# FFN-down projection: weight panels by column chunk, one sum of the seven-product square taken by an accumulating transfer, and four more squares

## The chip, the cores and the metric

The kernel runs on one core of a Trainium2 chip. The metric is the device time in microseconds (us) of one execution; lower is better. The engines named here are PE (matmul), DVE (vector), ACT (scalar), POOL (GpSimd) and SP (issues transfers).

## What is computed

One decoder layer over 256 tokens of width 2048, in float32. The change concerns the channel mixer:

```python
h2 = rms_norm(x, mlp_norm[i])
x = x + jnp.square(jax.nn.relu(h2 @ w_ffn_up[i])) @ w_ffn_down[i]   # 2048 -> 8192 -> 2048
gate = jax.nn.sigmoid(rms_norm(x, ple_norm[i]) @ w_ple_gate[i])
x = x + gate * (p[i] @ w_ple_proj[i])
```

## The kernel before

**Split numbers.** Each float32 operand is split into a high part `wh` (ACT copies it to the matmul's type, 512 columns at a time) and a low part `wl` (DVE subtracts the copy from the original). A product of two split operands takes three matmuls, high x high, high x low, low x high, on 128x512 tiles. Raw weights come as panels of 128x1024 (512 KB) by transfers that SP issues in order (`load_raw`, L158); six buffers go round, three in each of two pools.

**The down projection.** The hidden width 8192 is worked in two halves (`hf` 0 and 1), each after its part of the up projection. A half has two sweeps (`pair` 0 and 1, 1024 output columns each), so there are four: d00, d01, d10, d11. A sweep runs over 16 steps `kp`. A step multiplies a 2x2 block of activation tiles (a11, a12, a21, a22; two token tiles by two tiles of 128 hidden channels) with a 2x2 block of weights (w11, w12, w21, w22; two tiles of hidden channels by two chunks of 512 columns). It does so in one of two ways:

- A *classic* step takes eight products, 24 matmuls. Its two panels are each split once, into `wh`/`wl` a and b.
- A *square* takes seven products (Winograd's form of Strassen's scheme), 21 matmuls. It needs sums of the weight blocks (`td`, t1 to t4, by DVE, L1269 to L1272), and these are split as well: `wh`/`wl` b for the second panel, c and d for the sums, `wad` for w11. It also needs sums of the activations, S, made once in each half in the up projection (`activation_sums`).

Squares are the steps in `SEVEN` = (1, 3, 5, 7, 9, 11, 13) in d00, d01 and d10, and (1, 3, 7, 11) in d11: 25 of 64. The other steps are classic. Eight banks of PSUM collect the products over the sweep; after its last square the sums of banks go into the residual `x`, scaled by `s2` (L1249).

**Buffers.** `wh`/`wl` of kinds a, b and c go round three tiles each, d two in all (`graw`, which the kept gate panels share in d11), `wad` and `td` have one each. A conversion waits until PE has done with what stood in its tile, and a panel's load waits until the last instruction that reads its buffer's old panel is through.

**Order.** Apart from the part up to the output projection, a scheduler sets the order on each engine from the program's order and priorities; conversions have a high priority. Each engine runs its instructions strictly in that order, and SP too.

Of the kernel before, what the change touches and what calls it, by code (L numbers as in the profile page):

```python
# [9 lines left out]
F32 = mybir.dt.float32  # L10
F32R = mybir.dt.float32r
# [29 lines left out]
def trunk(  # L41
# [1114 lines left out]
    def inv_ms():  # L1156
        ss2 = rms_stat(xr, "n2")
        nc.vector.tensor_scalar(s2, ss2, 1.0 / D, NORM_EPS, op0=ALU.mult, op1=ALU.add)
        nc.vector.reciprocal(s2, s2)

# [27 lines left out]
    SEVEN = (1, 3, 5, 7, 9, 11, 13)  # L1188
    s_slots = (0, 2, 5)

    def activation_sums(box, kp, r):

        i = SEVEN.index(kp)
        if i % 2 == 0:
            st = a8(s_slots[i // 2], f"S{kp}", F32R) if i < 6 else fp.tile([128, 1024], F32R, tag="S", name=f"S{kp}")
            box[kp] = box[SEVEN[min(i + 1, len(SEVEN) - 1)]] = st
# [5 lines left out]
        nc.vector.tensor_tensor(s3, a11, a21, op=ALU.subtract)  # L1202
# [4 lines left out]
    def down_sweep(hf, pair, ys, sboxes, hooks=(), between=None, seven=SEVEN):  # L1207

        nm = f"d{hf}{pair}"
        hooks = dict(hooks)  # L1210
# [37 lines left out]
        def add(tt, c, src):  # L1248
            nc.vector.scalar_tensor_tensor(xs(tt, c), src, s2[:, tt : tt + 1], xs(tt, c), op0=ALU.mult, op1=ALU.add)  # L1249

        for q, kp in enumerate(((0, 2, 1, 4, 3, *range(5, 16)) if hf else (0, 2, 1, 4, 3, 6, 5, 8, 7, 10, 9, 12, 11, 14, 13, 15)) if pair else range(16)):
# [4 lines left out]
            rx, ry = (load_raw(w_down[pair, hf * 32 + 2 * kp + i], 1024, f"{nm}_{kp}_{i}") for i in range(2))  # L1256
            if kp in seven:
                i = SEVEN.index(kp)
                st = sboxes[kp][:, i % 2 * 1024 : i % 2 * 1024 + 1024]
                s1, s2_, s3, s4 = ((st[:, c * 128 : c * 128 + 128], st[:, 512 + c * 128 : 640 + c * 128]) for c in range(4))  # L1260
                t_ = a8(1, f"t{nm}_{kp}")
                t1, t3, t2, t4 = (t_[:, c * 512 : c * 512 + 512] for c in range(4))
                wa = fp.tile([128, 1024], F32R, tag="wa", name=f"wa{nm}_{kp}")
                w11 = wa[:, 0:512], wa[:, 512:1024]
                with tc.high_priority(20000):
                    split_sb(*w11, rx[:, 0:512])
                w21, w22 = halves_of(ry, f"{nm}_{kp}b")
                with tc.high_priority(20000):
                    nc.vector.tensor_tensor(t1, rx[:, 512:1024], rx[:, 0:512], op=ALU.subtract)  # L1269
                    nc.vector.tensor_tensor(t3, ry[:, 512:1024], rx[:, 512:1024], op=ALU.subtract)  # L1270
                    nc.vector.tensor_tensor(t2, t3, rx[:, 0:512], op=ALU.add)
# [213 lines left out]
```

## Time and profile before

| what | value |
|---|---|
| median of 3 runs | 1182.05 us (1179.92 to 1183.51) |
| span of the profiled execution | 1177.7 us (that execution's total time is not given) |
| busy PE, DVE, ACT, POOL | 1162.0, 872.0, 710.5, 13.9 us |
| sweeps d00 and d01, from the first matmul | 556.90 and 639.19 us |
| sweeps d10 and d11, from the first matmul | 899.9 and 982.2 us |
| HBM read | 213.59 MB |

The span runs from the first to the last instruction. Numbers of buffers are left out of names in the trace, so `wl_d_5c` is the low part of kind c at step 5 in any sweep. In a row of the timeline the columns are start, duration, engine, line, operation, out<-in, shapes, and in brackets the idle time before it and what ended that.

### The profile page before, as it was taken

The page shows a single profiled execution, that of the slowest core. Times are in us where ns is not written, and L with a number is a line of the kernel's source. Part 1 is how long each engine was busy: PE and PEld are TensorE (multiplying, and loading weights), DVE is VectorE, ACT ScalarE, POOL GpSimd, SP SyncE. Part 2 cuts the span into 40 slices and gives each one's busy share as a digit, 9 for nine tenths or more (in the row PEclk, how much of TensorE's full clock was granted, in tenths as well). Part 3 has the DMA queues.
Part 4 walks back from the last instruction along what each step waited for, and adds up shares of the span by engine and source line. Part 5 has one row for each costly group of instructions (what it writes and reads, how often), then busy time and mean ns, then how long its engine had stood idle before and what let it go on. Part 6 is the DMA issues. An engine that isn't in the chain of part 4 may idle for free.

```text
span 1177.7 us, 17287 instructions
## 1 busy us (share of the span) xinstructions
PE 1162.0 (99%) x6419; PEld 973.2 (83%) x6419; DVE 872.0 (74%) x1184; ACT 710.5 (60%) x1313; POOL 13.9 (1%) x73
## 2 busy tenths in 40 slices
PE   9999999999999999999999999999999999999997
PEld 8787777788887888888888888888888888888886
DVE  7686996954756666767988987666678979788543
ACT  8776858676545465555665664555556655668544
POOL 2100000000000000000000000000000000000000
PEclk9999999999999999999999999999999999999999
DMA  8464443354555555556556556555555556767511
GB/s 292 158 199 144 140 146 109 119 179 162 175 186 176 179 182 194 193 185 209 185 198 210 206 199 203 194 184 195 182 194 190 206 206 196 291 227 249 196 54 72
DMA packets 60756, 216.81 MB, mean 184 GB/s; under 512 B 6784, under 2 KB 7552, under 8 KB 60288
## 3 DMA queue, kind: packets, MB, share of 16 engines
q1 hardware_dynamic: 60240, 215.12, 54.3%
q8 instruction: 50, 0.82, 0.3%
q10 hardware_dynamic: 432, 0.60, 0.1%
q14 instruction: 34, 0.28, 0.1%
HBM read 213.59 MB, written 2.10 MB: 183 GB/s over the span
## 4 chain that ended last, share of the span: by engine, by line
PE 94%; ACT 2%; DVE 2%; DMA 1%; SPq 0%; issue 0%; DVEq 0%; ACTq 0%
PE u_w L1112 20%; PE u_w L1117 10%; PE d_b L1230 7%; PE d_b L1231 7%; PE d_b L1229 7%; PE d_w L1230 2%; PE d_w L1231 2%; PE d_w L1229 2%; PE gt_b L242 2%; PE gt_b L241 2%; PE gt_b L238 2%; PE o_b L241 1%; PE o_b L242 1%; PE zv_b L238 1%; PE o_b L238 1%; PE zp_b L238 1%
## 5 line engine op out<-in xcount | busy, mean ns | idle before, releaser
L1112 PE MATMUL u_w<-h,wh_u 128*128 128x512 f32 x1024 | 321.9, 396 | 0.0
L167 ACT ACTIVATE wh_u<-raw_u 128x512 fp32r<-128x512 f32 x256 | 147.5, 623 | 160.9 <-issue 98.2
L168 DVE TENSOR_TENSOR wl_u<-raw_u,wh_u 128x1024 fp32r<-128x1024 f32 x128 | 156.6, 1224 | 105.0 <-ACT wh_u L167 103.3
L1117 PEld LDWEIGHTS u_w<-h,wl_u 128*128 128x128 f32 x1024 | 192.4, 188 | 45.4
L1117 PE MATMUL u_w<-h,wl_u 128*128 128x256 f32 x1024 | 201.4, 278 | 0.0
L1112 PEld LDWEIGHTS u_w<-h,wh_u 128*128 128x128 f32 x1024 | 156.0, 189 | 0.1
L168 DVE TENSOR_TENSOR wl_gt<-raw_gt,wh_gt 128x1024 fp32r<-128x1024 f32 x24 | 29.4, 1224 | 23.2 <-ACT wh_gt L167 23.2
L167 ACT ACTIVATE wh_gt<-raw_gt 128x512 fp32r<-128x512 f32 x48 | 28.0, 638 | 23.1 <-PE gt_b L242 14.4
L241 PE MATMUL gt_b<-wh_gt,h 128*128 128x512 f32 x96 | 37.3, 389 | 0.0
L242 PE MATMUL gt_b<-wh_gt,h 128*128 128x512 f32 x96 | 37.3, 389 | 0.0
L168 DVE TENSOR_TENSOR wl_o<-raw_o,wh_o 128x1024 fp32r<-128x1024 f32 x16 | 19.6, 1223 | 12.9 <-ACT wh_o L167 9.9
L167 ACT ACTIVATE wh_o<-raw_o 128x512 fp32r<-128x512 f32 x32 | 18.4, 623 | 16.3 <-issue 8.4
L167 ACT ACTIVATE wh_zp<-raw_zp 128x512 fp32r<-128x512 f32 x32 | 18.6, 624 | 15.8 <-PE zp_b L242 7.2
L168 DVE TENSOR_TENSOR wl_zk<-raw_zk,wh_zk 128x1024 fp32r<-128x1024 f32 x16 | 19.4, 1222 | 9.2 <-ACT wh_zk L167 9.2
L241 PE MATMUL zv_b<-wh_zv,hTh 128*128 128x512 f32 x64 | 26.0, 406 | 0.0
L241 PE MATMUL zp_b<-wh_zp,hTh 128*128 128x512 f32 x64 | 25.7, 401 | 0.0
L238 PE MATMUL gt_b<-wl_gt,h 128*128 128x512 f32 x96 | 25.7, 389 | 0.0
L168 DVE TENSOR_TENSOR wl_zv<-raw_zv,wh_zv 128x1024 fp32r<-128x1024 f32 x16 | 19.5, 1221 | 8.2 <-ACT wh_zv L167 7.3
L241 PE MATMUL zk_b<-wh_zk,hTh 128*128 128x512 f32 x64 | 25.2, 394 | 0.3 <-ACT wh_zk L167 0.3
L241 PE MATMUL zr_b<-wh_zr,hTh 128*128 128x512 f32 x64 | 25.4, 397 | 0.0
L167 ACT ACTIVATE wh_zk<-raw_zk 128x512 fp32r<-128x512 f32 x32 | 18.4, 623 | 11.0 <-PE zv_b L242 4.0
L242 PE MATMUL zp_b<-wh_zp,hTl 128*128 128x512 f32 x64 | 25.0, 391 | 0.0
(837 smaller groups left out, 2964.2 us busy)
## 6 DMA issues: line engine op xcount, KB each, us to landing
raw_u<-in_w_ffn_up_dram SPq DMA_DIRECT2D x128, 512.0 KB, 3.5
raw_d<-in_w_ffn_down_dram SPq DMA_DIRECT2D x128, 512.0 KB, 4.3
raw_gt<-in_w_ple_gate_dram SPq DMA_DIRECT2D x24, 512.0 KB, 3.5
raw_zk<-in_w_in_dram SPq DMA_DIRECT2D x16, 512.0 KB, 3.6
raw_zr<-in_w_in_dram SPq DMA_DIRECT2D x16, 512.0 KB, 3.3
raw_zv<-in_w_in_dram SPq DMA_DIRECT2D x16, 512.0 KB, 3.4
raw_zp<-in_w_in_dram SPq DMA_DIRECT2D x16, 512.0 KB, 3.3
raw_o<-in_w_out_dram SPq DMA_DIRECT2D x16, 512.0 KB, 4.0
```

The lines of the kernel that those rows point to most:

```text
L167: nc.scalar.activation(wh[:, a * 512 : (a + 1) * 512], raw[:, a * 512 : (a + 1) * 512], AF.Copy)
L168: nc.vector.tensor_tensor(wl, raw, wh.bitcast(F32), op=ALU.subtract)
L238: nc.tensor.matmul(banks[tt], ah[:, ts_], halves[a][1], start=False, stop=last)
L241: nc.tensor.matmul(banks[tt], ah[:, ts_], halves[a][0], start=i + a == 0, stop=False)
L242: nc.tensor.matmul(banks[tt], al[:, ts_], halves[a][0], start=False, stop=False)
L1112: nc.tensor.matmul(bank[:, ct, :].rearrange("p (s t) -> p s t", s=2), wh[:, cs[ct]], hl, start=k == 0, stop=False, skip_group_check=True,)
L1117: nc.tensor.matmul(bank[:, ct, 0:T], wl[:, cs[ct]], hl[:, 0, :], start=False, stop=k == 15, skip_group_check=True)
L1229: nc.tensor.matmul(banks[n], ah, wh, start=first, stop=False)
L1230: nc.tensor.matmul(banks[n], ah, wl, start=False, stop=False)
L1231: nc.tensor.matmul(banks[n], al, wh, start=False, stop=last)
```

## The change

- The weights of the down projection are laid out by column chunk: the first panel of a step holds [w21, w11], the second [w22, w12], instead of one panel for each tile of hidden channels.
- In a square, after the second panel has landed, POOL issues an accumulating transfer that adds w11 from memory to the panel's half with w12 (256 KB). The panel then holds w22 and w11 + w12.
- One DVE subtraction of 512 columns makes t2 = (w11 + w12) - w22, and one of 1024 columns makes [w21 - t2, w11 - t2]. Before there were four of 512. Signs are changed: s3 is negated, and the sums that it enters are added with `ns2` = -`s2`.
- Both panels are split whole (a and b), the pair of differences is d, and t2 goes through `wad`. Kind c is gone.
- `SEVEN` becomes (1, 3, 4, 6, 8, 9, 11, 13), eight squares in d00, d01 and d10; d11 takes (1, 3, 6, 9, 11). That makes 29 of 64. The second sweeps run over the steps in another order (`visits`).
- The order of the products in a square changes (6, 4, 7 at the end), and classic steps take the panels by column chunk.
- `phl` of the next stage takes the tile of the last S.

```diff
-    SEVEN = (1, 3, 5, 7, 9, 11, 13)
+    SEVEN = (1, 3, 4, 6, 8, 9, 11, 13)
...
-        nc.vector.tensor_tensor(s3, a11, a21, op=ALU.subtract)
+        nc.vector.tensor_tensor(s3, a21, a11, op=ALU.subtract)
...
+        visits = (range(16), (0, 2, 1, 5, 3, 4, 7, 6, 10, 8, 9, 12, 11, 14, 13, 15))[pair] if seven is SEVEN else (0, 2, 1, 4, 3, *range(5, 16))
...
+        def panel(kp, c, name):
+            return load_raw(w_down[pair, hf * 16 + kp, c].rearrange("p r n -> p (r n)"), 1024, name)
...
-            rx, ry = (load_raw(w_down[pair, hf * 32 + 2 * kp + i], 1024, f"{nm}_{kp}_{i}") for i in range(2))
+            rx, ry = (panel(kp, c, f"{nm}_{kp}_{c}") for c in range(2))
...
+                nc.gpsimd.dma_start(ry[:, 512:1024], w_down[pair, hf * 16 + kp, 0, :, 1, :], accum_op=ALU.add)
                 t_ = a8(1, f"t{nm}_{kp}")
-                t1, t3, t2, t4 = (t_[:, c * 512 : c * 512 + 512] for c in range(4))
+                t2, t43 = t_[:, 0:512], t_[:, 512:1536]
                 wa = fp.tile([128, 1024], F32R, tag="wa", name=f"wa{nm}_{kp}")
-                w11 = wa[:, 0:512], wa[:, 512:1024]
+                w2 = wa[:, 0:512], wa[:, 512:1024]
+                w21, w11 = halves_of(rx, f"{nm}_{kp}a")
+                w22, w1 = halves_of(ry, f"{nm}_{kp}b")
                 with tc.high_priority(20000):
-                    split_sb(*w11, rx[:, 0:512])
-                w21, w22 = halves_of(ry, f"{nm}_{kp}b")
-                with tc.high_priority(20000):
-                    nc.vector.tensor_tensor(t1, rx[:, 512:1024], rx[:, 0:512], op=ALU.subtract)
-                    nc.vector.tensor_tensor(t3, ry[:, 512:1024], rx[:, 512:1024], op=ALU.subtract)
-                    nc.vector.tensor_tensor(t2, t3, rx[:, 0:512], op=ALU.add)
-                    nc.vector.tensor_tensor(t4, ry[:, 0:512], t2, op=ALU.subtract)
-                w1, w3 = halves_of(t_[:, 0:1024], f"{nm}_{kp}c")
-                w2, w4 = halves_of(t_[:, 1024:2048], f"{nm}_{kp}d", True)
-                for n, a_, w_ in (("1", a11, w11), ("2", a12, w21), ("3", s4, w22), ("5", s1, w1), ("7", s3, w3), ("6", s2_, w2), ("4", a22, w4)):
+                    nc.vector.tensor_tensor(t2, ry[:, 512:1024], ry[:, 0:512], op=ALU.subtract)
+                    nc.vector.tensor_tensor(
+                        t43.rearrange("p (r n) -> p r n", r=2), rx.rearrange("p (r n) -> p r n", r=2),
+                        t2.unsqueeze(1).to_broadcast([128, 2, 512]), op=ALU.subtract,
+                    )
+                    split_sb(*w2, t2)
+                w4, w3 = halves_of(t43, f"{nm}_{kp}d", True)
+                for n, a_, w_ in (("1", a11, w11), ("2", a12, w21), ("3", s4, w22), ("5", s1, w1), ("6", s2_, w2), ("4", a22, w4), ("7", s3, w3)):
                     prod(n, a_, w_)
...
-                    add(0, 1, u)
+                    add(0, 1, u, ns2)
...
-            down_sweep(hf, 1, ys, sboxes, {5: keep, 8: keep, 11: keep, 14: keep}, lambda: [h3_part("ple_norm", n) for n in range(2)], (1, 3, 7, 11))
+            down_sweep(hf, 1, ys, sboxes, {5: keep, 8: keep, 11: keep, 14: keep}, lambda: [h3_part("ple_norm", n) for n in range(2)], (1, 3, 6, 9, 11))
...
-    ph, pl = (fp.tile([128, 512], F32R, tag=nm, name=nm) for nm in ("ph", "pl"))
+    phl = fp.tile([128, 2048], F32R, tag="S", name="phl")
+    ph, pl = phl[:, 0:512], phl[:, 512:1024]
...
-        "w_ffn_down": a["w_ffn_down"][0].reshape(64, 128, 2, 1024).transpose(2, 0, 1, 3),
+        "w_ffn_down": a["w_ffn_down"][0].reshape(32, 2, 128, 2, 2, 512)[:, ::-1].transpose(3, 0, 4, 2, 1, 5),
```

What this does to the order of instructions is seen best on DVE. In the names, `raw_d00_8_1` is the second panel of step 8 in sweep d00 (0 is the first), `td` holds the sums of a square's weights, `wl_d00_8a` is the low part of kind a, and the last number is the buffer's. DVE in sweep d00 before, from square 5 to the beginning of square 7:

```order
L1269 TENSOR_TENSOR td00_5_5627<-raw_d00_5_0_5623 128x512
L1270 TENSOR_TENSOR td00_5_5627<-raw_d00_5_1_5625,raw_d00_5_0_5623 128x512
L1271 TENSOR_TENSOR td00_5_5627<-td00_5_5627,raw_d00_5_0_5623 128x512
L1241 TENSOR_TENSOR wl_d00_4a_5590<-raw_d00_4_0_5585,wh_d00_4a_5589 128x1024
L173 TENSOR_TENSOR wad00_5_5628<-raw_d00_5_0_5623,wad00_5_5628 128x512
L1241 TENSOR_TENSOR wl_d00_4b_5607<-raw_d00_4_1_5587,wh_d00_4b_5606 128x1024
L1272 TENSOR_TENSOR td00_5_5627<-raw_d00_5_1_5625,td00_5_5627 128x512
L1241 TENSOR_TENSOR wl_d00_5b_5632<-raw_d00_5_1_5625,wh_d00_5b_5631 128x1024
L1241 TENSOR_TENSOR wl_d00_5d_5646<-td00_5_5627,wh_d00_5d_5645 128x1024
L1241 TENSOR_TENSOR wl_d00_5c_5641<-td00_5_5627,wh_d00_5c_5640 128x1024
L1269 TENSOR_TENSOR td00_7_5713<-raw_d00_7_0_5709 128x512
L1270 TENSOR_TENSOR td00_7_5713<-raw_d00_7_1_5711,raw_d00_7_0_5709 128x512
```

The sums of a square stand between the conversions; each reads panels that have landed, and t1 needs the first panel alone.

DVE in sweep d00 now, from square 8 to the second panel of it (the subtraction of 9 is in between, since 8 and 9 are adjacent squares):

```order
L1276 TENSOR_TENSOR td00_8_5767<-raw_d00_8_1_5764 128x512
L1277 TENSOR_TENSOR td00_8_5767<-raw_d00_8_0_5762,td00_8_5767 128x1024
L1244 TENSOR_TENSOR wl_d00_7a_5729<-raw_d00_7_0_5724,wh_d00_7a_5728 128x1024
L1244 TENSOR_TENSOR wl_d00_7b_5746<-raw_d00_7_1_5726,wh_d00_7b_5745 128x1024
L1244 TENSOR_TENSOR wl_d00_8a_5770<-raw_d00_8_0_5762,wh_d00_8a_5769 128x1024
L173 TENSOR_TENSOR wad00_8_5768<-td00_8_5767,wad00_8_5768 128x512
L1244 TENSOR_TENSOR wl_d00_8d_5784<-td00_8_5767,wh_d00_8d_5783 128x1024
L1276 TENSOR_TENSOR td00_9_5814<-raw_d00_9_1_5811 128x512
L1277 TENSOR_TENSOR td00_9_5814<-raw_d00_9_0_5809,td00_9_5814 128x1024
L1244 TENSOR_TENSOR wl_d00_8b_5775<-raw_d00_8_1_5764,wh_d00_8b_5774 128x1024
```

Both subtractions of square 8 (L1276 reads the half that the added transfer completes) stand ahead of the two conversions of classic step 7, and those of 9 ahead of the second panel of 8.

The same queue further on, from square 11 to the first panel of step 12:

```order
L1276 TENSOR_TENSOR td00_11_5899<-raw_d00_11_1_5896 128x512
L1244 TENSOR_TENSOR wl_d00_10b_5878<-raw_d00_10_1_5858,wh_d00_10b_5877 128x1024
L1277 TENSOR_TENSOR td00_11_5899<-raw_d00_11_0_5894,td00_11_5899 128x1024
L1244 TENSOR_TENSOR wl_d00_11a_5902<-raw_d00_11_0_5894,wh_d00_11a_5901 128x1024
L173 TENSOR_TENSOR wad00_11_5900<-td00_11_5899,wad00_11_5900 128x512
L1244 TENSOR_TENSOR wl_d00_11d_5916<-td00_11_5899,wh_d00_11d_5915 128x1024
L1244 TENSOR_TENSOR wl_d00_11b_5907<-raw_d00_11_1_5896,wh_d00_11b_5906 128x1024
L1276 TENSOR_TENSOR td00_13_5984<-raw_d00_13_1_5981 128x512
L1277 TENSOR_TENSOR td00_13_5984<-raw_d00_13_0_5979,td00_13_5984 128x1024
L1244 TENSOR_TENSOR wl_d00_12a_5946<-raw_d00_12_0_5941,wh_d00_12a_5945 128x1024
```

Here one conversion of step 10 follows the subtraction of 11, and the conversions of step 12 follow both subtractions of 13.

DVE at the start of d00, now, right behind the first subtraction of square 1 (`r7` and `y7` belong to the end of the up projection):

```order
L1277 TENSOR_TENSOR td00_1_5465<-raw_d00_1_0_5460,td00_1_5465 128x1024
L1244 TENSOR_TENSOR wl_d00_0a_5427<-raw_d00_0_0_5422,wh_d00_0a_5426 128x1024
L173 TENSOR_TENSOR wad00_1_5466<-td00_1_5465,wad00_1_5466 128x512
L1244 TENSOR_TENSOR wl_d00_1d_5482<-td00_1_5465,wh_d00_1d_5481 128x1024
L1244 TENSOR_TENSOR wl_d00_0b_5444<-raw_d00_0_1_5424,wh_d00_0b_5443 128x1024
L1244 TENSOR_TENSOR wl_d00_1a_5468<-raw_d00_1_0_5460,wh_d00_1a_5467 128x1024
L1321 TENSOR_TENSOR r7_1_5410<-u7_w1_5317,r7_1_5410 128x512
L1322 SCALAR_TENSOR_TENSOR r7_1_5410<-r7_1_5410 128x512
L1244 TENSOR_TENSOR wl_d00_1b_5473<-raw_d00_1_1_5462,wh_d00_1b_5472 128x1024
L173 TENSOR_TENSOR y7_5217<-r7_1_5410,y7_5217 128x512
L1276 TENSOR_TENSOR td00_3_5550<-raw_d00_3_1_5547 128x512
L1244 TENSOR_TENSOR wl_d00_2a_5512<-raw_d00_2_0_5507,wh_d00_2a_5511 128x1024
```

The first subtraction of square 3 has moved ahead of the conversion of step 2's first panel; both stand behind square 1.

POOL after its last copy of the earlier stages, now (before, nothing followed there; `in_w_ffn_down_dram` is the weights in memory); the list goes on in the same way through the four sweeps:

```order
L804 COPY tE_t_2736<-AR1_1500 128x6x64 x2
L1268 DMA raw_d00_1_1_5462<-in_w_ffn_down_dram 128x512
L1268 DMA raw_d00_3_1_5547<-in_w_ffn_down_dram 128x512
L1268 DMA raw_d00_4_1_5594<-in_w_ffn_down_dram 128x512
L1268 DMA raw_d00_6_1_5679<-in_w_ffn_down_dram 128x512
L1268 DMA raw_d00_8_1_5764<-in_w_ffn_down_dram 128x512
```

Each of them waits for its panel's landing, and the DVE subtraction of L1276 waits for it.

24 lines of the change are left out of this document (13 added, 11 removed).

## The prediction

> **What bounds the kernel now.** I read the page's head and chain first: whether one engine carries the span.
>
> ```profile
> span 1177.7 us, 17287 instructions
> PE 1162.0 (99%) x6419; PEld 973.2 (83%) x6419; DVE 872.0 (74%) x1184; ACT 710.5 (60%) x1313; POOL 13.9 (1%) x73
> PE 94%; ACT 2%; DVE 2%; DMA 1%; SPq 0%; issue 0%; DVEq 0%; ACTq 0%
> ```
>
> PE carries the span. Then the busy times by stretch, for the four sweeps of the down projection (start:end, length, busy time of each engine).
>
> ```profile
> core 0: us, PE busy (x) PEld busy (x) DVE busy (x) ACT busy (x) POOL busy (x), PEclk, DMA share, GB/s
> 556.90:639.20 82.30, 82.30 (x366) 68.14 (x365) 71.37 (x83) 49.68 (x86) 0.00 (x0) 1.00 0.58 199
> 639.20:726.00 86.80, 86.80 (x390) 71.96 (x389) 76.42 (x87) 51.40 (x89) 0.00 (x0) 1.00 0.58 200
> 890.00:987.00 97.00, 97.00 (x444) 80.78 (x443) 86.06 (x100) 58.08 (x102) 0.00 (x0) 1.00 0.58 201
> 987.00:1060.00 73.00, 73.00 (x331) 60.26 (x330) 60.80 (x68) 47.17 (x87) 0.00 (x0) 1.00 0.70 249
> ```
>
> PE has no hole in any sweep, at full granted clock, and DVE runs beside it at 87 to 89% in the first three. Nothing else can become faster than PE's own instruction count allows; anything that comes late costs its full lateness. What one matmul costs is the spacing of starts, not the row's duration (matmuls overlap): first matmul of sweep d00 and first of d01.
>
> ```profile
> 556.90 0.40 PE L1229 MATMUL d_b<-wh_d_0a,y 128*128 128x512 f32 x1
> ...
> 639.19 0.39 PE L1229 MATMUL d_b<-wh_d_0a,y 128*128 128x512 f32 x1
> ```
>
> Between them lie 7 squares of 21 matmuls and 9 classic steps of 24, 363 in all: 82.29 / 363 = 0.2267 us each. A square is 4.76 us, a classic step 5.44 us, one product 0.68 us.
>
> **What the change takes from PE.** Squares go from 7+7+7+4 to 8+8+8+5, four more. Each replaces 24 matmuls by 21: 12 x 0.2267 = 2.7 us, the whole possible gain, 0.23%. Comparisons of this kernel tell about 0.3% (3.5 us) from no change.
>
> **What it takes from the converters.** One period of d00 on DVE, kp 5 (square) to kp 7 (the numbers in brackets are idle time):
>
> ```profile
> 581.48 1.23 DVE L1241 TENSOR_TENSOR wl_d_5c<-td,wh_d_5c 128x1024 fp32r<-128x1024 f32 x1 [1.17 <-ACT wh_d_5c L1240]
> 582.74 0.69 DVE L1269 TENSOR_TENSOR td<-raw_d 128x512 f32<-128x512 f32 x1
> 583.35 0.68 DVE L1270 TENSOR_TENSOR td<-raw_d,raw_d 128x512 f32<-128x512 f32 x1
> 584.07 0.69 DVE L1271 TENSOR_TENSOR td<-td,raw_d 128x512 f32<-128x512 f32 x1
> 584.68 1.22 DVE L1241 TENSOR_TENSOR wl_d_6a<-raw_d,wh_d_6a 128x1024 fp32r<-128x1024 f32 x1
> 585.81 0.69 DVE L173 TENSOR_TENSOR wad<-raw_d,wad 128x512 fp32r<-128x512 f32 x1
> 586.41 1.22 DVE L1241 TENSOR_TENSOR wl_d_6b<-raw_d,wh_d_6b 128x1024 fp32r<-128x1024 f32 x1
> 587.55 0.69 DVE L1272 TENSOR_TENSOR td<-raw_d,td 128x512 f32<-128x512 f32 x1
> 588.15 1.22 DVE L1241 TENSOR_TENSOR wl_d_7b<-raw_d,wh_d_7b 128x1024 fp32r<-128x1024 f32 x1
> ```
>
> Back to back a 512-column instruction takes 0.62 us of the queue and a 1024-column one 1.14. A square costs DVE five of the first and three of the second before, 6.5 us, and two and four after, 5.8 us; a classic step stays at 2.3. A sweep: 7 x 6.5 + 9 x 2.3 = 66 before, 8 x 5.8 + 8 x 2.3 = 65 after. ACT converts seven halves a square as before. The converters are no tighter over a sweep, and since PE never waits for them this saves nothing.
>
> Small things, at nothing:
>
> ```profile
> L1201 DVE TENSOR_TENSOR s<-r x14: 291/293/294, 404.6 to 881.4; 128x128 f32<-128x128 f32 x14
> L1158 DVE TENSOR_SCALAR s2sq<-ss_n x1: 164/164/164, 440.7 to 440.7; 128x2 f32<-128x2 f32 x1
> L168 DVE TENSOR_TENSOR wl_u<-raw_u,wh_u 128x1024 fp32r<-128x1024 f32 x128 | 156.6, 1224 | 105.0 <-ACT wh_u L167 103.3
> ```
>
> One more square in each half means one more set of activation sums, four of 0.29 us and a split, and once `ns2` at 0.16 us, all in the up projection, where DVE idles 105 us before `wl_u`. If that cover were gone they would cost 4 us. `phl` in the place of S waits for square 11's last product, some 20 us before it is needed.
>
> **What it adds: a transfer in series.** Per square, POOL waits for the second panel, issues an accumulating transfer of 256 KB into half of it, and DVE's first subtraction waits for that landing. POOL has nothing else to do there (0.00 in the stretches), so nothing is queued behind it but the next such transfer. Behind the subtraction on DVE, though, stand conversions that PE needs sooner, and the panel's buffer is freed later. Loads have no spare start: SP waits for the buffers.
>
> ```profile
> SPq L158 <- DVE wl_d_8a L1241: 23.9, 4, 6.3
> SPq L158 <- DVE wl_d_9b L1241: 8.7, 4, 4.7
> ```
>
> The issue waits up to 6.3 us for `wl_d_8a` to be done (us in total, times, longest). Six buffers go round, so the second panel of square n is issued when `wl` b of three steps earlier is done. The price X of the added transfer, from the issuable moment to landing, is in no row. Nearest rows (KB, median us to landing):
>
> ```profile
> raw_u<-in_w_ffn_up_dram SPq DMA_DIRECT2D x128, 512.0 KB, 3.5
> raw_d<-in_w_ffn_down_dram SPq DMA_DIRECT2D x128, 512.0 KB, 4.3
> gu<-in_g_up_dram SPq DMA_DIRECT2D x2, 256.0 KB, 4.2
> wa<-in_wa_up_dram SPq DMA_DIRECT2D x2, 256.0 KB, 2.8
> raw_pT<-in_pT_dram SPq DMA_DIRECT2D x1, 256.0 KB, 3.8
> ```
>
> Plain 256 KB transfers take 2.8 to 4.2 us. The new one adds a read of its destination, issued from another engine, so I keep 2.8 as the low end; for the high end, 5.0, the 4.2 of `gu` plus the 0.8 by which `raw_d` in a crowd exceeds `raw_u`. I take X = 3.8, the row of `raw_pT`: that size, in this part of the program, between panel loads. A panel load spaced from others is 3.5.
>
> **The place that repeats.** The pattern in d00 is 7 classic, 8, 9 squares, 10 classic, 11 square, 12 classic, 13 square; t2 is the first subtraction. Suppose t2 of 8 starts at s, late enough that PE waits for `wl_d00_7a` behind it. That ends at s + 0.62 + 1.14 + 1.2, and with 0.1 of signalling PE starts 7 at s + 3.05. It starts 9 at T = s + 3.05 + 5.44 + 4.76 = s + 13.25. DVE goes on without a break through `wl_d00_8b`, ten instructions, 3 x 0.62 + 7 x 1.14: done at s + 9.8 = T - 3.45. That frees the buffer for 11's second panel: landed T + 0.05, summed T + 0.05 + X. Does t2 of 11 wait? The instruction ahead, `wl_d00_9d`, follows an ACT conversion that waits for PE to finish 8, as here:
>
> ```profile
> 580.29 1.15 ACT L1240 ACTIVATE wh_d_5c<-td 128x512 fp32r<-128x512 f32 x2 [1.58 <-PE d_b L1231]
> ```
>
> So DVE is free at T + 0.3 + 1.15 + 1.2 = T + 2.7; the sum comes at T + 3.85. With 0.12 of signalling, t2 and `wl_d00_10b` end at T + 5.8, and 13's second panel is loaded: landed T + 9.35, summed T + 13.15; t2 of 13 starts at T + 13.25 and `wl_d00_12a` is ready 3.05 later, T + 16.3. PE is through 9, 10, 11 at T + 4.76 + 5.44 + 4.76 = T + 14.96. It waits 1.35 us. In general the wait is 2 (3.5 + X) - 13.25: zero at X = 3.1, twice as steep as X. It falls on 7 and 12 in d00 and in d10 and on the two like places in d01: 6 x 1.35 = 8.1 us.
>
> **The starts of sweeps.** In d00 the second panel of square 1 is what DVE waited for even before; its first reader:
>
> ```profile
> L1270 DVE TENSOR_TENSOR td<-raw_d,raw_d x25: 682/684/694, 549.3 to 1027.6; 128x512 f32<-128x512 f32 x25
> ```
>
> t2 now starts at 549.3 + 3.8 = 553.1; six instructions later `wl_d00_0b` is done at 558.9, which frees the buffer for square 3: landed 562.4, summed 566.2. `wl_d00_2a`, behind t2 of 3, is ready at 568.1, and PE wants it at 556.90 + 5.44 + 4.76 = 567.1: 1.0 us. From there seven DVE instructions to `wl_d00_3b` (both subtractions of 4 stand before it) end at 576.3, wanted at 575.0: 1.3 us. Twice, for d00 and d10: 4.6 us. In d01 and d11 the first squares come later, with 1 us more room in the same two round trips (2 x 7.3 - 14.2 = 0.4 us each); in d11 a one-round place gives 0.2 and square 11, whose last product shares buffers with the kept gate panels, 0.5. Together 1.5 us.
>
> **Sum.** -2.7 + 8.1 + 4.6 + 1.5 = +11.5 us. The page gives the span, 1177.7, and no total of that execution; the median of the runs is 4.3 above it, and I put the sum on the median, 1182.05: 1193.5.
>
> **Rivals.** *The transfer is hidden.* If X is at most 3.1, the repeating wait is gone, and at 2.8 only 0.5 in d11 remains: 1182.05 - 2.7 + 0.5 = 1179.9. For it: `wa` at 2.8, an idle POOL, DMA share of only 0.58. Against: the other two rows of that size. Decided at X = 3.1. The Trainium skill (DMA: Bandwidth & Descriptors, Anatomy of one DMA, SWDGE path) puts a transfer issued from POOL at about 2.0 us plus its bytes over 436 GB/s, which would be an estimated 2.6 us here and lead to this case; no run so far shows a transfer issued from POOL, and the rule says nothing of accumulation.
>
> *The transfer is much slower.* At X = 5 the repeating wait is 3.75, six times 22.5; the starts 7.5 for d00 and d10; d01 about 3, d11 about 5: 38 - 2.7 = +35, 1217. For it: 29 more transfers, 7.6 MB, on a queue share already at 0.58 to 0.70, and each reads and writes SBUF.
>
> *DVE becomes the bound by adjacent squares* (3, 4 and 8, 9), with X small: two squares cost DVE 11.6 us against PE's 9.5. But conversions run a step ahead, and over the five-step period DVE needs 22 of 25.2 us; it costs at most the 1.3 us at `wl_d00_3b` twice.
>
> **How the numbers follow.** Forecast case (X from 3.1 to 4.6, 0 to +27 us): 0.5. Hidden: 0.35, kept that high since the walk turns on a margin of 0.7 us in X. Much slower: 0.15. Hidden gives -2 us, a quarter of it read as faster: 0.09 faster, 0.26 same. Of the forecast case 0.07 lies under +3.5 (X below 3.3). So 0.09, 0.33, 0.58. The range takes in the hidden case with a run's scatter, 1177.5, and goes up to X = 4.5 (repeating wait 2.75, 16.5; starts 7.5; d01 and d11 5): 1209, with 5 for panel loads slowed by the traffic: 1214.
>
> **What would show it.** Right: PE idle in front of the products with `wh_d_7a`, `wh_d_12a` (d00), `wh_d_2a`, `wh_d_3b`, ended by DVE `wl_d`; DVE idle before L1276 ended by DMA `raw_d`; POOL's transfers near 3.8 us. Wrong: PE without holes in the sweeps and those transfers under 3.1; or, if PE waits while they are under 3.1, my walk of the queues. PE's matmuls must be 12 fewer in any case.

## The result, and the profile after

| | before | after |
|---|---|---|
| median of 4 runs each | 1182.35 us (1179.92 to 1183.51) | 1274.77 us (1271.28 to 1275.74) |
| ratio, 95% interval | | 1.0781 [1.0767, 1.0795] |
| span of the profiled execution | 1177.7 us | 1269.6 us |
| mean granted clock over the span | 0.998 | 0.976 |

The change costs 92 us. The forecast had 11, with 1214 as its upper end. The page of the changed kernel: head, granted clock by slices, the new queue, the shares of the chain (the work that ended last, followed back from the end), and the group of t2, the subtraction that reads the summed panel (busy, mean ns | idle before it, what ended it).

```profile
span 1269.6 us, 17391 instructions
PE 1190.7 (94%) x6407; PEld 985.4 (78%) x6407; DVE 871.9 (69%) x1161; ACT 716.6 (56%) x1327; POOL 39.1 (3%) x102
PEclk9999999999999999999888999999998998999999
q0 software_dynamic: 4176, 7.60, 3.7%
PE 71%; DMA 11%; DVE 8%; issue 7%; ACT 2%; SPq 0%; DVEq 0%; POOLq 0%; ACTq 0%
L1276 DVE TENSOR_TENSOR td<-raw_d 128x512 f32<-128x512 f32 x29 | 20.1, 692 | 106.9 <-DMA raw_d<-in_w_ffn_down_dram 83.4
```

PE has 12 matmuls fewer, and DVE is as busy as before (871.9 against 872.0), but it stands idle 106.9 us in front of t2, and the chain, once 94% PE, now goes through DMA, DVE and issue for 26%. Before, the four subtractions of all squares had 4.6 us of idle time in front of them, most of it at the first of them:

```profile
L1269 DVE TENSOR_TENSOR td<-raw_d 128x512 f32<-128x512 f32 x25 | 17.3, 692 | 2.4 <-DMA raw_d<-in_w_ffn_down_dram 1.8
```

In the two pairs of sweeps (stretch, length, busy times, granted clock, DMA share) PE no longer runs without holes:

```profile
557.50:763.50 206.00, 171.68 (x691) 136.01 (x690) 139.88 (x141) 100.16 (x177) 13.05 (x15) 0.93 0.60 178
946.60:1165.00 218.40, 189.39 (x785) 151.04 (x784) 154.19 (x163) 115.10 (x208) 10.45 (x12) 0.94 0.63 200
```

One wait, in sweep d00, step by step. PE first:

```profile
603.01 0.39 PE L1232 MATMUL d_b<-wh_d_7a,y 128*128 128x512 f32 x1
609.20 0.80 PE L1233 MATMUL d_b<-wl_d_7a,y 128*128 128x512 f32 x1 [5.80 <-DVE wl_d_7a L1244]
```

PE wants the low part of the first panel of step 7, a classic step. ACT had made the high part of it by 598.98:

```profile
597.84 1.14 ACT L1243 ACTIVATE wh_d_7a<-raw_d 128x512 fp32r<-128x512 f32 x2
```

So the panel had long landed. As far as the trace tells, DVE could have made `wl_d_7a` at 599.7, when it was through with `wl_d_6b`. Instead:

```profile
598.44 1.22 DVE L1244 TENSOR_TENSOR wl_d_6b<-raw_d,wh_d_6b 128x1024 fp32r<-128x1024 f32 x1
606.05 0.69 DVE L1276 TENSOR_TENSOR td<-raw_d 128x512 f32<-128x512 f32 x1 [6.40 <-issue]
606.78 1.22 DVE L1277 TENSOR_TENSOR td<-raw_d,td 128x1024 f32<-128x1024 f32 x1
607.92 1.22 DVE L1244 TENSOR_TENSOR wl_d_7a<-raw_d,wh_d_7a 128x1024 fp32r<-128x1024 f32 x1
```

t2 of square 8 is ahead of it in the queue and waits 6.4 us for the accumulating transfer, which POOL began at 598.72 and which landed at 605.97 ("issue" here means that the profile names no releaser; the landing is 0.08 us ahead of the start):

```profile
598.72 0.87 POOL L1268 DMA_DIRECT2D raw_d<-in_w_ffn_down_dram  x1 [12.33 <-DVE wl_d_6d L1244]
```

In 24 of the 29 squares t2 starts within 0.1 us of its transfer's landing. DVE's wait for these landings, and the three largest waits of PE, which end at low parts that stood behind a t2 (engine, what it waited for, us in total, times, longest):

```profile
DVE td L1276 <- DMA raw_d<-in_w_ffn_down_dram: 83.4, 18, 8.8
PE d_b L1233 <- DVE wl_d_7a L1244: 8.2, 2, 5.8
PE d_b L1233 <- DVE wl_d_2a L1244: 8.0, 2, 4.0
PE d_b L1233 <- DVE wl_d_12a L1244: 7.3, 2, 4.9
```

And the clock. The stretch inside and behind that wait (its columns as above, the granted clock third from the end):

```profile
600.00:606.40 6.40, 3.40 (x15) 2.45 (x14) 0.35 (x1) 1.17 (x3) 0.00 (x0) 1.00 0.49 125
607.00:610.30 3.30, 1.10 (x3) 0.91 (x4) 3.30 (x4) 1.62 (x3) 0.62 (x1) 0.50 0.58 84
610.50:617.00 6.50, 6.50 (x23) 5.17 (x23) 5.79 (x6) 1.28 (x3) 0.00 (x0) 0.75 0.70 239
```

Half the clock is granted from 607.0 to 613.8, 6.8 us; matmuls start 0.43 us apart there in place of 0.2267. The two pairs of sweeps have 12 such stretches, of 3.4 or 6.8 us.

The account, from the starts of successive matmuls: 27 gaps over 0.7 us cost 67.5 us beyond the usual spacing (36.8 in d00 and d01, 30.7 in d10 and d11), the matmuls at slower spacing some 25 us, 12 fewer matmuls give 2.7 back: some 90 of the 91.9 us between the spans.

### The profile page after: what moved, and what is told of

It reads as the page before. It is cut to its first block, busy times and chain, and to the rows that moved or that the text cites. A ratio compares the mean times of both kernels' runs of the same rounds, so it can differ in the third digit from the quotient of the medians.

```text
span 1269.6 us, 17391 instructions
## 1 busy us (share of the span) xinstructions
PE 1190.7 (94%) x6407; PEld 985.4 (78%) x6407; DVE 871.9 (69%) x1161; ACT 716.6 (56%) x1327; POOL 39.1 (3%) x102
## 3 DMA queue, kind: packets, MB, share of 16 engines
q0 software_dynamic: 4176, 7.60, 3.7%
## 4 chain that ended last, share of the span: by engine, by line
PE 71%; DMA 11%; DVE 8%; issue 7%; ACT 2%; SPq 0%; DVEq 0%; POOLq 0%; ACTq 0%
PE u_w L1112 17%; DMA raw_d<-in_w_ffn_down_dram 9%; PE u_w L1117 9%; PE d_b L1233 3%; PE d_b L1234 3%; PE d_b L1232 3%; PE gt_b L242 2%; PE gt_b L238 2%; PE gt_b L241 2%; PE o_b L241 1%; PE o_b L242 1%; PE zv_b L238 1%; PE o_b L238 1%; PE zp_b L238 1%; PE zv_b L241 1%
## 5 line engine op out<-in xcount | busy, mean ns | idle before, releaser
L1276 DVE TENSOR_TENSOR td<-raw_d 128x512 f32<-128x512 f32 x29 | 20.1, 692 | 106.9 <-DMA raw_d<-in_w_ffn_down_dram 83.4
L172 ACT ACTIVATE wad<-td 128x512 fp32r<-128x512 f32 x29 | 18.2, 628 | 68.5 <-DVE td L1276 61.5
L1268 POOL DMA_DIRECT2D raw_d<-in_w_ffn_down_dram x29 | 25.4, 875 | 833.7 <-DVE r L1322 490.6
L1277 DVE TENSOR_TENSOR td<-raw_d,td 128x1024 f32<-128x1024 f32 x29 | 35.4, 1222 | 0.5
L167 ACT ACTIVATE wh_o<-raw_o 128x512 fp32r<-128x512 f32 x32 | 18.4, 623 | 16.2 <-issue 8.4
```

The lines of the kernel that those rows point to most:

```text
L167: nc.scalar.activation(wh[:, a * 512 : (a + 1) * 512], raw[:, a * 512 : (a + 1) * 512], AF.Copy)
L1268: nc.gpsimd.dma_start(ry[:, 512:1024], w_down[pair, hf * 16 + kp, 0, :, 1, :], accum_op=ALU.add)
L1277: nc.vector.tensor_tensor(t43.rearrange("p (r n) -> p r n", r=2), rx.rearrange("p (r n) -> p r n", r=2), t2.unsqueeze(1).to_broadcast([128 ...
```

## Experiments

Theory A: the transfer in series, with t2 ahead of other work in DVE's queue. B: the squares' places and the new order of products. C: the added traffic on the DMA engines. The kernel before, run beside all of these, had medians from 1180.3 to 1181.7; each ratio is against the runs that it shared.

| kernel | us | ratio, 95% interval |
|---|---|---|
| e1, DVE makes the sum | 1187.94 | 1.0070 [1.0052, 1.0088] |
| e3, 25 squares of before, transfer kept | 1274.11 | 1.0784 [1.0764, 1.0803] |
| e4, plain transfer | 1242.33 | 1.0515 [1.0488, 1.0541] |
| e5, DVE's sum and the transfers beside | 1194.36 | 1.0109 [1.0092, 1.0125] |
| e3b, 25 squares, DVE's sum | 1193.87 | 1.0107 [1.0090, 1.0124] |
| e7, DVE's sum, d11 with four squares | 1188.43 | 1.0068 [1.0054, 1.0082] |
| e8, half a transfer | 1253.78 | 1.0623 [1.0595, 1.0651] |
| e9, e3 with seven panel buffers | 1244.77 | 1.0548 [1.0528, 1.0567] |
| e13, t2 later in DVE's queue | 1203.17 | 1.0182 [1.0161, 1.0204] |
| e14, e13 with b in two pieces | 1200.79 | 1.0167 [1.0153, 1.0181] |
| e2, no sum | 1182.45 | 1.0012 [1.0003, 1.0021] |
| e17, e14 with no sum | 1192.49 | 1.0094 [1.0081, 1.0107] |
| e18, e14 on e9 | 1190.43 | 1.0077 [1.0064, 1.0090] |
| e12, DVE's sum, b in two pieces | 1181.28 | 1.0001 [0.9992, 1.0010] |
| e16, e12 with d11 as before | 1181.46 | 1.0004 [0.9994, 1.0014] |

### e1: the sum by DVE

```diff
-                nc.gpsimd.dma_start(ry[:, 512:1024], w_down[pair, hf * 16 + kp, 0, :, 1, :], accum_op=ALU.add)
+                with tc.high_priority(20000):
+                    nc.vector.tensor_tensor(ry[:, 512:1024], ry[:, 512:1024], rx[:, 512:1024], op=ALU.add)
```

> The changed kernel with the accumulating transfer undone: DVE adds w11 to the half with w12 (one more 512-column instruction a square, 0.62 us, 29 in all), everything else as in the changed kernel: panels by column chunk, 29 squares, order of the steps. Theory A (the transfer stands in series between a panel's landing and DVE's first subtraction, so PE waits, and after a wait it runs at half the granted clock for some us): the waits go, no granted clock of 0.5 inside the sweeps, 1180 us (1177 to 1186), that is 2.7 us of matmuls less than before. Theory B (eight squares in this order cannot be fed by DVE and ACT whatever makes the sum): still over 1210 us, waits before wh_d_7a, wh_d_12a remain. Theory C (traffic of the transfers slows the panel loads): 1180 as well, told apart by e5_beside.

Measured 1187.94, 2 us above theory A's range, far from theory B's. Without the transfer 87 of the 92 us are gone, though DVE has 29 additions more. The 6 us that stay above the kernel before are small waits at b panels and two in d11 (PEld is PE's weight load):

```profile
PEld d_b L1233 <- DVE wl_d_6d L1244: 2.4, 1, 2.4
PEld d_b L1233 <- DVE wl_d_11d L1244: 2.3, 1, 2.3
```

### e3: the squares and steps of before, transfer kept

```diff
-    SEVEN = (1, 3, 4, 6, 8, 9, 11, 13)
+    SEVEN = (1, 3, 5, 7, 9, 11, 13)
...
-        visits = (range(16), (0, 2, 1, 5, 3, 4, 7, 6, 10, 8, 9, 12, 11, 14, 13, 15))[pair] if seven is SEVEN else (0, 2, 1, 4, 3, *range(5, 16))
+        visits = (range(16), (0, 2, 1, 4, 3, 6, 5, 8, 7, 10, 9, 12, 11, 14, 13, 15))[pair] if hf == 0 else ((0, 2, 1, 4, 3, *range(5, 16)) if pair else range(16))
```

> The changed kernel with the squares and the orders of steps of before (7, 7, 7 and 4, squares and classic steps by turns), the accumulating transfer kept. Theory A: with the transfers at 4.4 to 7 us my walk of the queues gives 33 to 95 us of waits and some 15 of lower clock: 1215 to 1290 us. Theory B: the squares were the trouble, so 1182 us (1179 to 1190).

(The last sweep's squares go back to those of before as well.) Measured 1274.11, the same as with 29 squares. The squares' places are not the cause, and with e1 B falls for the bulk of the loss: the new order of products stands in e1 too.

### e4: a plain transfer in the same place

```diff
-                nc.gpsimd.dma_start(ry[:, 512:1024], w_down[pair, hf * 16 + kp, 0, :, 1, :], accum_op=ALU.add)
+                nc.gpsimd.dma_start(ry[:, 512:1024], w_down[pair, hf * 16 + kp, 0, :, 1, :])
```

> The changed kernel with a plain transfer from POOL in place of the accumulating one: same place, bytes, queue and waits, but w11 replaces the half instead of being added, so the sum is left out of the computation. Theory A in two forms. A1 (the price is the way: issue by POOL, and packets queued among those of panel loads): from landing of the panel to landing of the transfer still 4 to 8 us, 1250 to 1275 us. A2 (the price is the accumulation, reading the destination): under 3.5 us, 1185 to 1215 us.

Measured 1242.33, between the ranges of A1 and A2. The accumulation is a third of the loss (32 of 92 us), the plain transfer in the series most of the rest. The rows of the transfers (KB, median us from POOL's start to landing), after:

```profile
raw_d<-in_w_ffn_down_dram POOLq DMA_DIRECT2D x29, 256.0 KB, 5.4
```

and plain, with the row of its queue:

```profile
raw_d<-in_w_ffn_down_dram POOLq DMA_DIRECT2D x29, 256.0 KB, 4.1
q0 software_dynamic: 2320, 7.60, 1.9%
```

The fastest of the 29 took 3.79 us with the addition and 2.80 without. The accumulating queue has 4176 packets for 7.60 MB, 144 for each transfer, the plain one 80.

### e5: the same transfers, but nobody waits for them

```diff
+                a_ = aside[:, i % 2 * 512 : i % 2 * 512 + 512]
+                nc.gpsimd.tensor_copy(a_[:, 0:1], ry[:, 0:1])
+                nc.gpsimd.dma_start(a_, w_down[pair, hf * 16 + kp, 0, :, 1, :], accum_op=ALU.add)
```

(Lines beside DVE's sum of e1; `aside` is a spare tile, and the copy makes the transfer start after the panel's landing.)

> DVE makes the sum as in e1_dve_sum, and the 29 accumulating transfers are still issued after each second panel's landing, into a spare tile that nobody reads (POOL copies one column of the panel first, to be held back like the transfer). Theory A (it is the wait in series): as e1_dve_sum within 3 us, some 1181 us. Theory C (the traffic, through slower panel loads): over 1210 us.

Measured 1194.36, 6.4 us over e1. The traffic costs something, twice the 3 us that theory A allowed, but it is no rival to the series: C holds 6 of 92 us, as far as traffic beside DVE's sum tells.

### e3b, e7: what is left with DVE's sum

e3b joins the edits of e3 and e1.

> The squares and the order of the visits of the kernel before (25 squares), the new formulas, and VectorE forming w11 + w12 or its like in the panel itself, with no transfer on POOL. Theory 'only the transfer, with a rest from adjacent squares and from the kept gate panels': the rest of the 29-square kernel with VectorE's sum (1187.9, of which some 4.6 us stand in two waits of the sweep that also loads gate panels) goes away with the squares' places; 25 squares give 1180 to 1185. Rival 'the new formulas themselves cost' (products 5, 6, 4 and 7 need the sum, then t2, then the double subtraction in a row, where before product 5 needed one subtraction): 1186 to 1193 with the old places too.

Measured 1193.87, at the upper end of the rival's range (0.9 us above it): slower than e1, with the places of before. PE waits in it at `wl_d_5b`, `wl_d_7b` and `wl_d_11b`:

```profile
PEld d_b L1233 <- DVE wl_d_5b L1244: 3.4, 3, 1.3
PEld d_b L1233 <- DVE wl_d_11b L1244: 2.6, 3, 1.0
PEld d_b L1233 <- DVE wl_d_7b L1244: 2.6, 3, 1.1
```

The sum stands ahead of the conversion of the whole second panel, so product 3, which needs no sum, waits too. e7 is e1 with

```diff
-            down_sweep(hf, 1, ys, sboxes, {5: keep, 8: keep, 11: keep, 14: keep}, lambda: [h3_part("ple_norm", n) for n in range(2)], (1, 3, 6, 9, 11))
+            down_sweep(hf, 1, ys, sboxes, {5: keep, 10: keep, 11: keep, 15: keep}, lambda: [h3_part("ple_norm", n) for n in range(2)], (1, 3, 8, 13))
```

> The 29-square kernel with VectorE's sum, but the last sweep has four squares at 1, 3, 8 and 13 in place of five at 1, 3, 6, 9 and 11, and its gate panels are loaded at visits 5, 10, 11 and 15 in place of 5, 8, 11 and 14, so that no square that shares the two gate buffers follows straight on such a load: 28 squares. Theory 'the two waits of 2.35 and 2.29 us and the half clock of 3.4 us behind one of them come from that sharing': they go, one square costs 0.68 us more of products: 1187.9 - 4.6 - 1.7 + 0.7 = 1182 (1179 to 1184.5). If the waits only move to another place of the sweep: 1186 to 1191. Under 1180 it would be at the kernel before or better.

Measured 1188.43, in the range of waits that only move. The two waits of d11 went, and others came behind the sweep's end (1.3 and 1.6 us, with 3.4 us at half clock), for the closing sums (L1252) and what is made of them; that the late square 13 pushed these back was not tried by itself.

### e8, e9: the price of the transfer, and its lead

e8 transfers 256 columns of w11 into `ry[:, 512:768]` and leaves the other half of the sum out.

> The changed kernel with half of each accumulating transfer: 256 of the 512 columns, 128 rows as before, so half of the bytes in as many packets; the sum of the other columns is left out. Quiet transfers took 3.8 to 4.3 us from POOL's start to the landing. Theory 'a fixed part rules (POOL's instruction, the first packet, one packet for each row, the add's way there and back)': quiet transfers 3.3 to 3.9 us, the kernel 1258 to 1275. Theory 'the bytes rule': quiet transfers 2.4 to 3.0 us, some 1.3 us off each of 27 waits and fewer stretches of half clock, 1210 to 1240.

Measured 1253.78, between the two expectations, and the fastest transfers took 3.04 us against 3.79: between them too. From the two minima, 1.5 us goes with the 256 KB and 2.3 us is there whatever the size (an estimate). This did not decide what rules; both parts count.

e9 is e3 with the change below, and with the last tile of the activation sums (and `phl`) half as large to make room:

```diff
-            own = len(deep) > 5 and len(deep) % 6 < 3
+            own = len(deep) > 5 and len(deep) % 7 < 4
...
-            raw = fp.tile([128, 1024], F32, tag="raw2", bufs=3, name=f"raw_{name}")
+            raw = fp.tile([128, 1024], F32, tag="raw2", bufs=4, name=f"raw_{name}")
```

> The changed formulas and the accumulating transfer on the squares and visits of the kernel before (1274.1 with six panel buffers), now with seven panel buffers in place of six; room for the seventh from the sums' last tile, 4 KB a partition wide in place of 8. A panel is issued one panel earlier, half a visit, 1.8 to 2.7 us. Theory 'the transfer stands in series with the load of its panel, and what counts is how early the panel lands': each of some 25 waits is shortened by about 1.5 to 2.2 us and fewer stretches of half clock follow: 1274 - 25 x 1.8 - some 10 = 1219 (1200 to 1240). Rival 'the crowding of POOL's transfer by the panel loads rules, whenever they come': 1260 to 1280.

Measured 1244.77, 5 us above the range of "how early the panel lands": one panel more of lead is worth 29 us. That points to the series, but says nothing on where in the series.

### e13: t2 later in DVE's queue

```diff
-                w22, w1 = halves_of(ry, f"{nm}_{kp}b")
-                with tc.high_priority(20000):
+                with tc.issue_after(low[0].ins):
+                    w22, w1 = halves_of(ry, f"{nm}_{kp}b")
+                with tc.high_priority(20000), tc.issue_after(low[0].ins):
```

`low[0]` is the last low part made, here that of the square's own first panel: t2 and what follows it on DVE are issued behind it, not ahead of the classic step's panels.

> The changed kernel (1274.8) with one thing else: VectorE's queue. t2 (the first operation that needs the accumulating transfer), the subtraction behind it and the halves of the second panel are issued behind the halves of the square's own first panel, in place of ahead of the halves of the panels before it. Everything else, the transfer included, is as it was. Theory 'the price is the place in VectorE's queue': PE's long waits (6.2, 5.3, 5.1, 4.3 us and so on) end at the low halves of a plain panel that had landed and stood behind t2; now PE has 12 to 24 more matmuls (2.7 to 5.4 us) to do while t2 waits, and each wait of some 2.8 us mean shrinks to under 1: 1274.8 - 25 x 2 - some 15 of half clock = 1210 (1190 to 1230). Theory 'the price is the transfer itself, wherever t2 stands' (PE would then wait as long at the second panel's halves): 1255 to 1280.

Measured 1203.17, in the range of the queue's theory: 71.6 of the 92 us are gone, with the same 29 transfers, which took a little longer than after:

```profile
raw_d<-in_w_ffn_down_dram POOLq DMA_DIRECT2D x29, 256.0 KB, 5.9
L1279 DVE TENSOR_TENSOR td<-raw_d 128x512 f32<-128x512 f32 x29 | 19.8, 684 | 0.0
```

t2 (now L1279) idles 0.0 us in all, against 106.9. The place shown above, now on DVE:

```profile
589.31 1.23 DVE L1246 TENSOR_TENSOR wl_d_6b<-raw_d,wh_d_6b 128x1024 fp32r<-128x1024 f32 x1 [3.07 <-ACT wh_d_6b L1245]
590.45 0.68 DVE L1279 TENSOR_TENSOR td<-raw_d 128x512 f32<-128x512 f32 x1
591.05 1.22 DVE L1246 TENSOR_TENSOR wl_d_7a<-raw_d,wh_d_7a 128x1024 fp32r<-128x1024 f32 x1
```

DVE still waits for a transfer in front of `wl_d_6b` (3.07 us, through ACT), but PE has products in hand. And the transfer of square 8, begun at 598.72 after, is begun at 591.28 here:

```profile
591.28 0.87 POOL L1270 DMA_DIRECT2D raw_d<-in_w_ffn_down_dram  x1 [9.90 <-DVE td L1279]
```

So the traces read as a loss that fed itself: DVE stuck at t2 converted landed panels late, their buffers came free late, the next square's panel was loaded and summed late, and DVE stuck again. The new edges bind DVE alone, but two more orders moved with them. The scheduler now lets PE start products of the next step ahead of a square's last ones: half of the matmuls of 7a, and some of 7b and 8a, come between the first matmul with t2 of square 6 (`wad`) and the other two. ACT makes `wh_d_8b` ahead of `wad` and `wh_d_8d`, where it came behind both. The three orders were not taken apart, so what the 71.6 us show is the price of the order on all three engines, with the transfers as they were.

### e14, e2, e17, e18: the rest

e14 adds to e13 that the second panel is converted in two pieces, the half without the sum first:

```diff
+                    nc.scalar.activation(w22[0], ry[:, 0:512], AF.Copy)
+                    low[0] = nc.vector.tensor_tensor(w22[1], ry[:, 0:512], w22[0].bitcast(F32), op=ALU.subtract)
+                with tc.high_priority(20000), tc.issue_after(low[0].ins):
+                    split_sb(*w1, ry[:, 512:1024])
```

> As the run before, and the second panel's halves are made in two pieces: the half that needs no sum first, then the sum's half, then t2 and the rest. So product 3 (1.36 us on PE) no longer waits for the transfer, and product 5 waits only for the sum's half. Queue theory: another 1 to 1.5 us off each wait that is left: 1183 to 1205. Transfer theory: 1245 to 1275.

Measured 1200.79, inside the range of the queue's theory, but only 2.4 us better. Product 3 is three matmuls, 0.68 us, and not the 1.36 us that was expected. e2 takes the line of the transfer out of the changed kernel, so that w11 is not added at all:

> The changed kernel with the sum left out altogether: no transfer, no addition, the panel's last quarter is taken as it was loaded. The floor of the change: 12 fewer matmuls, 2.7 us, two shorter formulas. If only the sum costs: 1178 to 1181. If the order of the products and the neighbouring squares cost too: 1183 to 1188.

Measured 1182.45. Between the two expectations: 3.9 us above the floor of 1178.6 (the kernel before beside it, 1181.28, less 2.7), with two waits at the end of d11 (2.4 and 2.1 us). e17 takes the same line out of e14:

> The kernel with t2 late in VectorE's queue and the second panel's halves in two pieces (1200.8), with the sum left out altogether: no transfer, no addition. If what is left of the loss (19 us) is the transfer's lateness: 1179 to 1184, as the changed kernel without a sum (1182.5). If the order itself costs (t2 and the halves of t4 and t3 come later in VectorE's queue whether there is a transfer or not): 1190 to 1200.

Measured 1192.49, in the range of an order that costs. The order of e14, the second panel in two pieces included, costs 10.0 us against e2 with no transfer to wait for, and the transfer, on top of that order, 8.3 us. The 10 us stand in the sweeps as many small waits of PE for what is made of t2, which now comes late even without a transfer, for `wad` above all:

```profile
PEld d_w L1233 <- DVE wad L173: 5.9, 9, 2.3
```

From the starts of matmuls, late starts in front of the products with `wad` and d sum up to 9.4 us in e17 and 2.7 in e2. e18 makes the edits of e14 on e9:

> The transfer kept, t2 late in VectorE's queue, the second panel's halves in two pieces, on the squares and visits of the kernel before (25 squares) with seven panel buffers. If the rest of the loss (1200.8 with six buffers) is lateness of the transfer, one panel more of lead takes most of it: 1183 to 1191. If the traffic or the order makes the rest: 1196 to 1204.

Measured 1190.43, in the range of lateness. Against e9 the later order takes 54.3 us off; with 29 squares (e14) it took 74.0. With 25 squares and one panel more of lead no more is left than in e17 with no transfer at all, so the 8.3 us look like lateness rather than traffic; squares and buffers changed together here, so this is not shown.

### e12, e16: can the gain be had?

e12 is e1 with the second panel in two pieces and d11 rearranged; with 28 squares, 9 matmuls fewer, 2.0 us could be gained:

```diff
+                    split_sb(*w22, ry[:, 0:512])
+                    nc.vector.tensor_tensor(ry[:, 512:1024], ry[:, 512:1024], rx[:, 512:1024], op=ALU.add)
+                    split_sb(*w1, ry[:, 512:1024])
...
-            down_sweep(hf, 1, ys, sboxes, {5: keep, 8: keep, 11: keep, 14: keep}, lambda: [h3_part("ple_norm", n) for n in range(2)], (1, 3, 6, 9, 11))
+            down_sweep(hf, 1, ys, sboxes, {5: keep, 6: keep, 12: keep, 14: keep}, lambda: [h3_part("ple_norm", n) for n in range(2)], (1, 3, 8, 11))
```

> VectorE's sum in place of the transfer (1187.9 with 29 squares), with the second panel's halves in two pieces, so that product 3 does not wait for the sum, and with the last sweep's squares at 1, 3, 8 and 11 and its gate panels at visits 5, 6, 12 and 14, so that none comes between two squares: 28 squares. Theory 'the rest over the kernel before is waits at the second panel's halves (0.6 to 1.3 us each) and at the two squares beside a gate panel': 1178 to 1182. If VectorE itself is short (29 more additions of 0.69 us, 20 us, in sweeps where it has about that to spare): 1184 to 1190.

Measured 1181.28, in the first theory's range and equal to the kernel before. d00 and d01 are whole again, and shorter by the six matmuls that they save:

```profile
557.40:720.40 163.00, 163.00 (x722) 134.97 (x721) 152.53 (x177) 101.25 (x177) 0.00 (x0) 1.00 0.63 209
```

163.0 us against 164.4 from first to last start. What it gains there goes at the end of d11, where PE waits 1.3 us for an activation of the next stage:

```profile
1056.10 0.66 PE L1134 MATMUL h3t<-ident,x 128*128 128x128 f32 x4 [1.26 <-DVE h L1141]
```

e16 is e12 with square 7 in place of 8, and d11 with the squares and the gate panels of before.

> VectorE's sum with the second panel's halves in two pieces (1181.3 with squares 8, 8, 8 and 4), with square 7 in place of 8 in all sweeps and the gate panels back at visits 5, 8, 11 and 14, so that the last sweep has the squares and the gate panels of the kernel before (1, 3, 7, 11): 28 squares. If the waits of 1.65 and 1.18 us at the end of the last sweep come from the gate panels' new places, they go: 1181.3 - 2 = 1179.3, and at or just under the kernel before (1178.5 to 1181). If they come from the new formulas: 1181 to 1184.

Measured 1181.46: no better, with waits of 0.8 us at two places in d10 and of 1.8 at the end of d11; the latter thus does not come from the gate panels' places. No version beat the kernel before.

## Why the prediction was wrong

**Mechanism: right; places: in part.** The prediction put the loss on the added transfer in series and named conversions behind t2 on DVE, and four places. PE did wait at `wl` of 7a, 12a and 2a, not at 3b. It also waited at steps that the walk had cleared. By the terms of the sum (us; measured are the gaps over 0.7 us, beyond the usual spacing):

| term | predicted | measured |
|---|---|---|
| 12 fewer matmuls | -2.7 | -2.7 |
| 7a and 12a in d00 and d10 | 5.4 | 16.2 |
| starts of d00 and d10 (2a, 3b) | 4.6 | 8.3 |
| d01 (two places like 7a and 12a, and its start) | 3.1 | 16.0 |
| d11 | 1.1 | 15.4 |
| other places in d00 and d10 | 0 | 11.6 |
| matmuls at slower spacing | 0 | some 25 |

**The step that failed: the price X**, the time from the second panel's landing to that of the accumulating transfer. The sum took 3.8 from `raw_pT`. POOL starts 0.56 to 0.73 us after the panel's landing, and from its start the transfers took 3.79 to 7.87 us, median 5.4 by the row above: X is 4.4 to 8.5, median 6.1. The high end of 5.0 that I had kept was too low: 17 of 29 lie above. Three things were missing.

- POOL's 0.56 to 0.73 us: the rows that X was taken from run from the issue, not from the landing that is waited for.
- An accumulating transfer takes 1.0 us longer than a plain one (3.79 against 2.80, the fastest of each), which stood in no row.
- The spread in a crowd. Beside panel loads the transfer stretches: 12 of 29 took up to 4.33 us, the rest 4.78 to 7.87. A sign of this stood in the view of the kernel before, where I gave 2.8 to 4.2 us for plain transfers of 256 KB and left out the row with 4.9; and its panel loads of 512 KB in the down projection, median 4.3, reached from 3.3 to 8.6 us.

```profile
xq<-in_xT_dram SPq DMA_DIRECT2D x1, 256.0 KB, 4.9
```

Of the 17 long ones 13 had a panel load issued within 0.84 us before or after POOL's start; the nearest load of any of the 12 short ones was 0.91 us away. That is no full account: two transfers, each with one load issued 1.91 us before it and one 0.96 us after, took 3.89 and 7.25 us. That the loads cause the stretch was seen, not tried by itself. The Trainium skill (DMA: Bandwidth & Descriptors, Anatomy of one DMA, SWDGE path) gives an estimated 2.6 us for this size; the fastest plain transfer, 2.80, comes near it, the accumulating ones do not.

**The formula held in kind, not in size.** With X = 6.1 the repeating wait is 2 (3.5 + 6.1) - 13.25 = 5.95 us. Measured beyond the usual spacing: 5.96 at 7a and 5.06 at 12a in d00, 2.59 and 2.57 in d10. That 5.95 meets 5.96 is luck: with the transfers' own times (X of squares 11 and 13 is 8.06 and 6.12 in d00, 7.00 and 4.60 in d10) the formula gives 7.9 and 5.4 us at 12a, some 2.8 us too much both times. The walk has PE run from 7a to 12a at full clock and without another wait; in both sweeps it did neither.

**The starts of sweeps, +4.6**, were 1.0 us at 2a and 1.3 at 3b in d00 and d10; measured 4.1 and 4.2 us at 2a, none at 3b. In *much slower*, 7.5 us for these starts at X = 5 is what the walk gives at 4.5; at 5 it gives 9.4.

**d01 and d11** were the worst terms. I walked these sweeps with X = 3.8, where their first squares have 1 us more room; at 6.1 the same formula, 2 (3.5 + X) - 14.2, gives 5.0 us for each, and 4.8 (5a) and 4.9 us (4a) were measured. The waits of d11 at 8b and 10a, 4.3 and 4.0 us, were priced at less than 1 us.

**A term that was missing: the clock.** Some 25 of the 92 us are matmuls at slower spacing, nearly all at half the clock, in stretches like the one from 607.0 to 613.8. The prediction priced a late wait at its lateness alone. The Trainium skill has this (TensorE: Matmul & The Clock Gate, Part 1): the clock is halved after at least one idle window of some 3.4 us, and the windows run freely. The lengths of 3.4 and 6.8 us agree, and all 12 stretches begin on one grid with a step of 3.413 us; "at least one idle window" does not quite, as a gap of 2.80 us at 1027.2 also brought 3.4 us at half clock, while one of 2.81 at 993.9 brought none. On the grid the two differ: the first lies in one window, with 2.4 us idle, the second is cut by a border, with 1.8 us idle before it. In this trace a window at full clock with 2.25 us idle or more was always followed by half clock, one with 1.8 or less never.

**Right:** 12 fewer matmuls (6407); DVE no tighter (871.9 us busy); the small things in the up projection cost nothing (sweep d00 starts 0.6 us later than before); no bound by adjacent squares, as e1, which has them, is faster than e3b, which has not (1187.94 and 1193.87).

**The rivals.** *Much slower* was the one that came, by its own mechanism, but its 1217 at X = 5 lacked the clock, most of d01 and d11, and the larger X. *Hidden* needed X up to 3.1, and the smallest was 4.4.

**What stays open:** how the 71.6 us of e13 split between the orders on DVE, ACT and PE; what stretches a transfer; and the wait at the end of d11 that takes back the gain in e12 and e16.

## What to carry to other kernels

When a change puts a transfer in series, look first at what stands behind its first reader on that engine. Here the scheduler had put the reader ahead of work that was ready, on an engine that runs in strict order, and most of the loss lay in the order (72 of 92 us went with an edge of order, which moved PE's and ACT's order too). Price a transfer of a new kind by the crowd that it runs in, not by a lone row of its size, and count from the event that it waits for. Where a wait's formula has a slope of two in that price, carry the high end through every sweep. Add the half clock after gaps of some 3 us or more: some 25 us here on 67 us of gaps.

## What was not expected of the hardware

- An accumulating transfer of 256 KB issued by POOL took at least 3.79 us from POOL's start, a plain one 2.80, half of the columns 3.04; it makes 144 packets in place of 80.
- Beside panel loads the same transfer took up to 7.87 us, and when nobody waited for the transfers (e5), all of the added traffic cost 6.4 us.
- A gap of 5 to 6 us on PE was followed by up to 6.8 us at half clock; over all gaps the slow matmuls added more than a third to them (some 25 us on 67).
- In the changed kernel's trace the stretches of half clock begin on one grid of 3.413 us, and what counted was the idle time inside a window of this grid, not the length of the gap.
